# MLP of a decoder trunk on one core: two products accumulate on in the banks of two others, five sums per pair in place of seven, and the products with a weight piece's remainder come last

## The chip, the core and the metric

The kernel runs on 1 core of one Trainium2 chip. The metric is the device time of one execution in microseconds (us). Three timed runs of the kernel before gave 2285.32 to 2286.46 us, with a median of 2285.71 us. Lower is better.

## What is computed

The reference is a decoder trunk of two layers over 256 tokens of width 2048: attention with an MLP behind it, then a state-space mixer with another MLP behind it. The change lies in the MLP alone, which runs twice:

```python
D_MODEL, SEQ, D_FF = 2048, 256, 8192

def squared_relu_mlp(h, w_in, w_out):      # h: (256, 2048), after an RMS norm
    u = jax.nn.relu(h @ w_in)              # (256, 8192)
    return (u * u) @ w_out                 # (256, 2048), added to the residual stream
```

All tensors are float32. The kernel keeps the precision by splitting each operand in two: a rounded part and the remainder, `(ah, al)` of the activations and `(wh, wl)` of the weights. A product of two operands is then three matmuls, `ah·wh + al·wh + ah·wl`, into one float32 accumulator.

## The kernel before, in words

**Weight pieces.** Weights come from HBM in pieces of 128x1024 float32 (512 KB: two blocks of 128 rows by 512 columns). The SP queue loads each into a raw buffer (`wraw`, six of them; `wrx`, four more in the MLP). ScalarE (ACT) rounds the piece into `wh` (L102), VectorE (DVE) subtracts to get the remainder `wl` (L103), and TensorE (PE) takes both. There are four `wh` and four `wl` buffers. `Flow.next` (L124) hands one piece to PE and converts up to three pieces ahead, so each piece goes DMA, ACT, DVE, PE. The PE program stands in the order of the code. The order on ACT and DVE is made by a scheduler when the program is built.

**The first matmul of the MLP.** The hidden layer is made in 16 column blocks of 512, taken two at a time: a pair `p` holds the blocks `2p` and `2p+1`. Pair 0 is computed straightforwardly (tokens of kind "c"). Pairs 1 to 7 use a 2x2 scheme of the Strassen kind: the tokens are cut into two halves of 128, the 2048 inputs into two halves of 1024, the pair into its two blocks, and seven products of half size stand for eight. They are called M1, N7, N5, N6, N4, M2, N3. Each takes four pieces (d = 0 to 3, tokens of kind "s") and accumulates over them in a PSUM bank of its own, six from the four banks of the pool `acc` in turn and N7 from the pool `sm`. In the profile a bank of such a product is called `st`. The activations that they multiply (sums and differences of the input's quarters) are made once per layer by `combinations`; the weights that they multiply are made from the loaded quarters by `seven`: DVE adds (L183) and, for two of them, adding DMAs of the GpSimd queue (L199).

**The sums behind the products.** When a product's fourth piece is done, `after` (L627) queues what can be made: ACT copies M1 out of its bank (L630); after N5 and N6, DVE makes w = N6 − m1, c = N5 + w, w = N7 + w and e = N7 + c (L636 to L639); after N4 it makes w − N4, after M2 it adds M2 to m1, after N3 it adds N3 to c. These are seven DVE sums per pair (L620 and L621 are the helpers that the profile names). e, w − N4, m1 + M2 and c + N3 are the four quarters of the pair's hidden values. Each goes through a Relu on ACT (L624), a square (L566), and a transposition on PE, whose result is split into `k` tiles (L299 on ACT, L300 on DVE) for the second matmul.

**The second matmul.** Tokens of kind "o" multiply the hidden values of an earlier pair with four pieces of the output weights, both token halves at once, into two banks of the pool `yp`; DVE then adds the result to the residual (L436). `merged` (L1415) mixes the "s" tokens of a pair with the "o" tokens of the pairs before it into one order, by a rough model of time, and `plan` (L1460) strings the pairs together. Neither is touched by the change.

**The products of one piece.** `products` (L609) issues the matmuls of one piece: six for an "s" token, twelve for a "c" or "o" token. Its order is, for each of the two row blocks and each accumulator: ah·wh (L616), ah·wl (L617), al·wh (L618). Outside these tokens, `block` (L328) does the same work in another order: all products with `wh` of the piece (L339, L340), then those with `wl` (L343).

Of the kernel before, what the change touches and what calls it, by code (L numbers as in the profile page):

```python
# [23 lines left out]
AF = mybir.ActivationFunctionType  # L24
# [5 lines left out]
S = 256  # L30
# [184 lines left out]
class Trunk:  # L215
# [343 lines left out]
    def mlp_body(self, mp, layer, gain):  # L559
        nc = self.nc  # L560
        xa, rs = self.xT, self.rs
        us = {}

        def hidden(r, pp, j, t):

            nc.scalar.activation(r, r, AF.Square)  # L566
            if (pp, j) not in us:
                us[pp, j] = (self.ktile(self.k4), self.ktile(self.k4))
            h, lo = us[pp, j]
            if by_words(pp, j, t):  # L570
                r = self.words(r, 3, mp)
            return lambda wide: self.transposes(r, h, lo, t, wide)

        def relu(src, t):
            r = self.scratch()
            nc.scalar.activation(r, src, AF.Relu, scale=rs[t])
            return r

        def lhs_x(kt, t):
            return [v[:, kt % 8] for v in xa[kt // 8, t]]  # L580

        def lhs_u(pp):
            return self.from_tiles([us[pp, 0], us[pp, 1]])

        S, steps = self.combinations(mp, xa)
        S["M1"], S["N4"], S["M2"] = xa[0, 0], xa[1, 1], xa[1, 0]
        out, bank, v, count = {}, {}, {}, {}
        due = []
        at = [0.0, 0.0]

        def when(us, fn):
            due.append((at[0] + us, fn))

        def move(us):
            at[0] += us
            for e in [e for e in due if e[0] <= at[0]]:
                due.remove(e)
                e[1]()

        def turn(r, p, j, t, us):  # L600

            fn = hidden(r, p, j, t)
            at[1] = max(at[0] + us + (COPY if by_words(p, j, t) else 0), at[1] + TR_GAP)
            due.append((at[1], lambda: fn(False)))

        def pair_of_banks(pool):
            return [pool.tile([P, 512], F32, tag=pool.name, name=self.name(pool.name)) for _ in range(2)]

        def products(accs, key, lhs, kt, first, last):  # L609
            u, (h, lo) = self.flow.next(key)  # L610
            for q in range(2):
                k = 2 * kt + q
                wh, wl = h[:, q * 512:(q + 1) * 512], lo[:, q * 512:(q + 1) * 512]
                for t, b in enumerate(accs):
                    ah, al = lhs(k, t)
                    nc.tensor.matmul(b, ah, wh, start=first and q == 0, stop=False)  # L616
                    nc.tensor.matmul(b, ah, wl, start=False, stop=False)  # L617
                    nc.tensor.matmul(b, al, wh, start=False, stop=last and q == 1)  # L618

        sub = lambda o, a, b: nc.vector.tensor_tensor(o, a, b, ALU.subtract)  # L620
        plus = lambda o, a, b: nc.vector.tensor_tensor(o, a, b, ALU.add)  # L621

        def relu_in_place(r, t):
            nc.scalar.activation(r, r, AF.Relu, scale=rs[t])  # L624
            return r

        def after(name, p):  # L627
            if name == "M1":
                v["m1"] = self.scratch()
                nc.scalar.activation(v["m1"], bank["M1"], AF.Copy)  # L630
            elif name in ("N5", "N6"):
                v[name] = p
                if v.get("N5") != p or v.get("N6") != p:
                    return
                w, c, e = (self.scratch() for _ in range(3))
                sub(w, bank["N6"], v["m1"])  # L636
                plus(c, bank["N5"], w)
                plus(w, bank["N7"], w)
                plus(e, bank["N7"], c)  # L639
                v["w"], v["c"] = w, c  # L640
                turn(relu_in_place(e, 1), p, 1, 1, TR[0])
            elif name == "N4":
                sub(v["w"], bank["N4"], v["w"])
                turn(relu_in_place(v["w"], 1), p, 0, 1, TR[1])
            elif name == "M2":
                plus(v["m1"], bank["M2"], v["m1"])
                turn(relu_in_place(v["m1"], 0), p, 0, 0, TR[2])
            elif name == "N3":
                plus(v["c"], bank["N3"], v["c"])
                turn(relu_in_place(v["c"], 0), p, 1, 0, TR[3])  # L650

        tokens = plan()
        inside = False
        when(5, steps[0])
        when(10, steps[1])
        for tok in tokens:
            key = (tok[0], layer) + tok[1:]
            if tok[0] == "s":
                _, p, name, d = tok
                if not inside:  # L660
                    inside = True
                    self.flow.ahead = (6, 3)
                if count.setdefault(name, 0) % 4 == 0:
                    pool = self.sm if name == "N7" else self.acc
                    bank[name] = pool.tile([P, 512], F32, tag=pool.name, name=self.name("st"))
                count[name] += 1
                products([bank[name]], key, lambda k, t: [x[:, k] for x in S[name]], d,
                         count[name] % 4 == 1, count[name] % 4 == 0)
                if count[name] % 4 == 0:
                    after(name, p)  # L670
                move(1.36)
            elif tok[0] == "c":
                _, p, j, o = tok
                if o == 0:
                    out["c"] = pair_of_banks(self.yp if j else self.acc)
                products(out["c"], key, lhs_x, o, o == 0, o == 7)
                if o == 7:
                    for t in range(2):
                        turn(relu(out["c"][t], t), p, j, t, TR[4])
                    if j:  # L680
                        when(3, steps[2])
                if o % 2:
                    self.tick()
                move(2.72)
            else:
                _, p, nb, o = tok
                if o == 0:
                    out[nb] = pair_of_banks(self.yp)
                products(out[nb], key, lhs_u(p), o, o == 0, o == 3)
                if o == 3:  # L690
                    self.add_residual(nb, out.pop(nb))
                move(2.72)
        move(1e9)
        assert not self.queue
        if gain is not None:
            self.boundary_begin(gain)
        for nb in range(4):
            keys = [("mo", layer, 7, nb, q) for q in range(2)]
            if gain is None and nb == 3:
                self.last_block(keys, lhs_u(7))  # L700
                break
            accs = self.block(keys, lhs_u(7))
            if gain is not None:
                self.finalize(nb, accs)
            else:
                for t in range(2):
                    self.result(t, nb, slice(0, 512), accs[t])
        if gain is not None:
            self.boundary_end()
# [694 lines left out]
TR = (10, 8, 7, 7, 5)  # L1404
# [4 lines left out]
def by_words(p, j, t):  # L1409

    return 0 < p < 7
# [48 lines left out]
def plan():  # L1460

    out = [("c", 0, 0, o) for o in range(8)]
    for p in range(1, 8):
        first = [(("o", p - 2, 3), 4)] if p > 1 else [(("c", 0, 1), 8)]
        out += merged(p, first + [(("o", p - 1, nb), 4) for nb in range(4 if p == 7 else 3)])
    return out
# [139 lines left out]
```

## Time and profile before

| what | value |
|---|---|
| timed runs, median (lowest to highest) | 2285.71 us (2285.32 to 2286.46) |
| span of the profiled execution, first to last instruction | 2284.5 us |
| PE busy | 2278.1 us, 10929 matmuls |
| DVE busy | 1915.9 us |
| ACT busy | 1390.1 us |
| granted TensorE clock | 1.000 |
| HBM read | 529.65 MB |

For the profiled execution the profile gives no other time of its own than this span; the median of the timed runs is 1.2 us above it, which is what lies before the first and behind the last instruction together with the spread of the runs (1.1 us).

How to read it: PE rows are matmuls, PEld rows are the loads of their stationary operand, which overlap the matmul before. Matmuls are pipelined, so a matmul's own duration (about 0.39 us) is longer than the distance from one start to the next (about 0.23 us), and the busy time of PE does not tell by itself whether it runs at its best. The idle time before an instruction is listed with what ended it.

### The profile page before, as it was taken

The page shows a single profiled execution, that of the slowest core. Times are in us where ns is not written, and L with a number is a line of the kernel's source. Part 1 is how long each engine was busy: PE and PEld are TensorE (multiplying, and loading weights), DVE is VectorE, ACT ScalarE, POOL GpSimd, SP SyncE. Part 2 cuts the span into 40 slices and gives each one's busy share as a digit, 9 for nine tenths or more (in the row PEclk, how much of TensorE's full clock was granted, in tenths as well). Part 3 has the DMA queues.
Part 4 walks back from the last instruction along what each step waited for, and adds up shares of the span by engine and source line. Part 5 has one row for each costly group of instructions (what it writes and reads, how often), then busy time and mean ns, then how long its engine had stood idle before and what let it go on. Part 6 is the DMA issues. An engine that isn't in the chain of part 4 may idle for free.

```text
span 2284.5 us, 30768 instructions
## 1 busy us (share of the span) xinstructions
PE 2278.1 (100%) x10929; PEld 1889.6 (83%) x10929; DVE 1915.9 (84%) x2318; ACT 1390.1 (61%) x1947; POOL 275.5 (12%) x315
## 2 busy tenths in 40 slices
PE   9999999999999999999999999999999999999999
PEld 7898888888888888888888888888888888888887
DVE  7786698999898897687899688676989889989985
ACT  7775576566666666564666555545666666666663
POOL 1440000000000000100133213121000000000000
PEclk9999999999999999999999999999999999999999
DMA  8545678888888878667888787767688888888874
GB/s 315 173 153 159 211 230 267 259 255 270 264 255 259 267 232 271 227 208 241 277 280 278 245 275 264 229 222 229 204 265 248 259 270 253 260 275 247 267 232 160
DMA packets 167706, 557.16 MB, mean 244 GB/s; under 512 B 19040, under 2 KB 28192, under 8 KB 166528
## 3 DMA queue, kind: packets, MB, share of 16 engines
q1 hardware_dynamic: 151264, 502.44, 66.2%
q0 software_dynamic: 13888, 48.49, 10.0%
q10 hardware_dynamic: 2400, 4.27, 0.5%
q8 instruction: 86, 1.41, 0.3%
q14 instruction: 68, 0.56, 0.1%
HBM read 529.65 MB, written 6.41 MB: 235 GB/s over the span
## 4 chain that ended last, share of the span: by engine, by line
PE 96%; DVE 1%; DMA 1%; ACT 1%; issue 1%; POOL 0%; SPq 0%; ACTq 0%; DVEq 0%
PE acc L339 13%; PE acc L340 13%; PE acc L343 13%; PE yp L618 9%; PE yp L617 9%; PE yp L616 9%; PE st L617 7%; PE st L618 7%; PE st L616 7%; DMA wraw<-mi 1%; PE sm L324 1%; DVE wl L103 1%; PE y L1309 1%; PE sm L322 1%; PE acc L616 1%; PE acc L618 1%
## 5 line engine op out<-in xcount | busy, mean ns | idle before, releaser
L102 ACT ACTIVATE wh<-wraw 128x1024 fp32r<-128x1024 f32 (+1 forms) x818 | 856.2, 1053 | 570.4 <-PE acc L340 268.9
L103 DVE TENSOR_TENSOR wl<-wraw,wh 128x1024 fp32r<-128x1024 f32 (+1 forms) x818 | 985.5, 1221 | 240.6 <-ACT wh L102 216.6
L616 PE MATMUL yp<-wh,k 128*128 128x512 f32 x896 | 349.2, 390 | 0.0
L618 PE MATMUL yp<-wh,k 128*128 128x512 f32 x896 | 348.8, 389 | 0.0
L617 PE MATMUL yp<-wl,k 128*128 128x512 f32 x896 | 348.6, 389 | 0.0
L339 PE MATMUL acc<-wh,xt 128*128 128x512 f32 x704 | 279.7, 397 | 0.4 <-ACT wh L102 0.4
L340 PE MATMUL acc<-wh,xt 128*128 128x512 f32 x704 | 274.9, 390 | 0.1
L102 ACT ACTIVATE wh<-wrx 128x1024 fp32r<-128x1024 f32 x168 | 177.8, 1058 | 153.4 <-PE yp L618 101.7
L103 DVE TENSOR_TENSOR wl<-wrx,wh 128x1024 fp32r<-128x1024 f32 x168 | 204.3, 1221 | 36.6 <-ACT wh L102 35.6
L618 PEld LDWEIGHTS yp<-wh,k 128*128 128x128 f32 x896 | 168.2, 188 | 35.1
L617 PEld LDWEIGHTS yp<-wl,k 128*128 128x128 f32 x896 | 168.2, 188 | 34.9
L616 PEld LDWEIGHTS yp<-wh,k 128*128 128x128 f32 x896 | 168.2, 188 | 34.8
L339 PE MATMUL acc<-wh,k 128*128 128x512 f32 x496 | 196.5, 396 | 0.0
L340 PE MATMUL acc<-wh,k 128*128 128x512 f32 x496 | 193.3, 390 | 0.0
L343 PE MATMUL acc<-wl,xt 128*128 128x512 f32 x704 | 188.3, 389 | 0.0
L616 PE MATMUL st<-wh,xt 128*128 128x512 f32 x448 | 177.7, 397 | 0.0
L618 PE MATMUL st<-wh,xt 128*128 128x512 f32 x448 | 174.9, 390 | 0.0
L617 PE MATMUL st<-wl,xt 128*128 128x512 f32 x448 | 174.7, 390 | 0.0
L339 PEld LDWEIGHTS acc<-wh,xt 128*128 128x128 f32 x704 | 132.7, 188 | 29.4 <-ACT wh L102 1.6
L340 PEld LDWEIGHTS acc<-wh,xt 128*128 128x128 f32 x704 | 132.5, 188 | 28.5 <-issue 1.2
L343 PEld LDWEIGHTS acc<-wl,xt 128*128 128x128 f32 x704 | 132.1, 188 | 27.7
L199 POOL DMA_DIRECT2D wrx<-mi x56 | 49.2, 878 | 720.6 <-DVE wl L103 524.5
(318 smaller groups left out, 3527.0 us busy)
## 6 DMA issues: line engine op xcount, KB each, us to landing
wraw<-mi SPq DMA_DIRECT2D x256, 512.0 KB, 5.5
wraw<-mo SPq DMA_DIRECT2D x256, 512.0 KB, 5.6
wraw<-si SPq DMA_DIRECT2D x160, 512.0 KB, 5.2
wraw<-so SPq DMA_DIRECT2D x64, 512.0 KB, 5.2
wrx<-mi SPq DMA_DIRECT2D x56, 512.0 KB, 5.4
wrx<-mi POOLq DMA_DIRECT2D x56, 512.0 KB, 7.8
wraw<-wo SPq DMA_DIRECT2D x32, 512.0 KB, 4.0
taps<-xD SPq DMA_DIRECT2D x16, 768.0 KB, 8.4
```

The lines of the kernel that those rows point to most:

```text
L102: self.last = nc.scalar.activation(h[:, v], raw[:, v], AF.Copy)
L103: self.last_lo = nc.vector.tensor_tensor(lo[:, v], raw[:, v], h[:, v].bitcast(F32), ALU.subtract)
L199: nc.gpsimd.dma_start(st["b11"].tile, quarter(d, 1, 0), accum_op=ALU.add)
L322: self.nc.tensor.transpose(b.bitcast(F32R)[:, v], words[:, v], self.ident_r)
L324: self.nc.tensor.transpose(b[:, v], src[:, v], self.ident)
L339: nc.tensor.matmul(accs[t][:, :n], ah, wh[:, q, :], start=first and kt + q == 0, stop=False)
L340: nc.tensor.matmul(accs[t][:, :n], al, wh[:, q, :], start=False, stop=False)
L343: nc.tensor.matmul(accs[t][:, :n], lhs(kt + q, t)[0], wl[:, q, :], start=False, stop=en and q == nk - 1)
L616: nc.tensor.matmul(b, ah, wh, start=first and q == 0, stop=False)
L617: nc.tensor.matmul(b, ah, wl, start=False, stop=False)
L618: nc.tensor.matmul(b, al, wh, start=False, stop=last and q == 1)
L1309: nc.tensor.matmul(y[t][c, o], part(t)[:, c], xg[g][t][:, o], start=True, stop=True)
```

## The change

The diff has two parts.

```diff
         def products(accs, key, lhs, kt, first, last, more=False):
             u, (h, lo) = self.flow.next(key)
+            half = lambda w, q: w[:, q * 512:(q + 1) * 512]
             for q in range(2):
-                k = 2 * kt + q
-                wh, wl = h[:, q * 512:(q + 1) * 512], lo[:, q * 512:(q + 1) * 512]
                 for t, b in enumerate(accs):
-                    ah, al = lhs(k, t)
-                    nc.tensor.matmul(b, ah, wh, start=first and q == 0, stop=False)
-                    nc.tensor.matmul(b, ah, wl, start=False, stop=False)
-                    nc.tensor.matmul(b, al, wh, start=False, stop=last and q == 1)
+                    ah, al = lhs(2 * kt + q, t)
+                    nc.tensor.matmul(b, ah, half(h, q), start=first and q == 0, stop=False, skip_group_check=more)
+                    nc.tensor.matmul(b, al, half(h, q), start=False, stop=False, skip_group_check=more)
+            for q in range(2):
+                for t, b in enumerate(accs):
+                    nc.tensor.matmul(b, lhs(2 * kt + q, t)[0], half(lo, q), start=False, stop=last and q == 1,
+                                     skip_group_check=more)
...
-                w, c, e = (self.scratch() for _ in range(3))
+                w, g, e = (self.scratch() for _ in range(3))
                 sub(w, bank["N6"], v["m1"])
-                plus(c, bank["N5"], w)
-                plus(w, bank["N7"], w)
-                plus(e, bank["N7"], c)
-                v["w"], v["c"] = w, c
+                plus(g, bank["N7"], w)
+                plus(e, bank["N5"], g)
+                v["w"], v["g"] = w, g
                 turn(relu_in_place(e, 1), p, 1, 1, TR[0])
             elif name == "N4":
-                sub(v["w"], bank["N4"], v["w"])
-                turn(relu_in_place(v["w"], 1), p, 0, 1, TR[1])
+                sub(v["g"], bank["N4"], v["g"])
+                turn(relu_in_place(v["g"], 1), p, 0, 1, TR[1])
             elif name == "M2":
-                plus(v["m1"], bank["M2"], v["m1"])
-                turn(relu_in_place(v["m1"], 0), p, 0, 0, TR[2])
+                nc.scalar.activation(v["m1"], bank["M1"], AF.Relu, scale=rs[0])
+                turn(v["m1"], p, 0, 0, TR[2])
             elif name == "N3":
-                plus(v["c"], bank["N3"], v["c"])
-                turn(relu_in_place(v["c"], 0), p, 1, 0, TR[3])
+                plus(v["w"], bank["N5"], v["w"])
+                turn(relu_in_place(v["w"], 0), p, 1, 0, TR[3])
...
-                if count.setdefault(name, 0) % 4 == 0:
+                onto = {"M2": "M1", "N3": "N5"}.get(name, name)
+                if count.setdefault(name, 0) % 4 == 0 and onto == name:
...
-                products([bank[name]], key, lambda k, t: [x[:, k] for x in S[name]], d,
-                         count[name] % 4 == 1, count[name] % 4 == 0)
+                products([bank[onto]], key, lambda k, t: [x[:, k] for x in S[name]], d,
+                         count[name] % 4 == 1 and onto == name, count[name] % 4 == 0, onto != name)
```

First, `products` issues all products with `wh` of a piece and then those with `wl`, as `block` does. Second, M2 accumulates on in the bank of M1, and N3 in that of N5: M1's bank is read by the copy in the middle and by a Relu of ACT at the end, so that M1 + M2 needs no DVE sum; N5's bank is read by e = N5 + g in the middle and by w + (N5 + N3) at the end, so that c is not made. Five sums are left, and a pair takes four `acc` banks in place of six. `skip_group_check` adds no instruction.

On PE the order within a piece changes. This is the first N6 piece of the fourth pair in the first layer (`st` is N6's bank, `sN` the activations' two parts, `wh` and `wl` the piece), before:

```order
L616 MATMUL st_5600<-wh_5551,sN_428_3186 128x512
L617 MATMUL st_5600<-wl_5552,sN_428_3186 128x512
L618 MATMUL st_5600<-wh_5551,sN_429_3187 128x512
L616 MATMUL st_5600<-wh_5551,sN_428_3186 128x512
L617 MATMUL st_5600<-wl_5552,sN_428_3186 128x512
L618 MATMUL st_5600<-wh_5551,sN_429_3187 128x512
```

and with the change:

```order
L615 MATMUL st_5588<-wh_5539,sN_428_3186 128x512
L616 MATMUL st_5588<-wh_5539,sN_429_3187 128x512
L615 MATMUL st_5588<-wh_5539,sN_428_3186 128x512
L616 MATMUL st_5588<-wh_5539,sN_429_3187 128x512
L619 MATMUL st_5588<-wl_5540,sN_428_3186 128x512 x2
```

The piece's remainder was read by the second matmul and is now first read by the fifth. In a piece of the "o" kind, with twelve matmuls, it was the second and is now the ninth.

On DVE the sums behind N5 and N6 of the third pair in the first layer (`s` is a scratch tile, `st` a bank: N6, N5, N7, N7 in turn) stood so before, between pieces' remainders:

```order
L620 TENSOR_TENSOR s_519_5266<-st_4893,s_518_5194 128x512
L103 TENSOR_TENSOR wl_5281<-wraw_5222,wh_5280 128x1024
L621 TENSOR_TENSOR s_520_5267<-st_4880,s_519_5266 128x512
L103 TENSOR_TENSOR wl_5295<-wraw_5234,wh_5294 128x1024
L621 TENSOR_TENSOR s_519_5266<-st_4838,s_519_5266 128x512
L621 TENSOR_TENSOR s_521_5268<-st_4838,s_520_5267 128x512
```

and stand so now (N6, N7, N5):

```order
L622 TENSOR_TENSOR s_515_5258<-st_4885,s_514_5186 128x512
L103 TENSOR_TENSOR wl_5271<-wraw_5214,wh_5270 128x1024
L623 TENSOR_TENSOR s_516_5259<-st_4830,s_515_5258 128x512
L103 TENSOR_TENSOR wl_5285<-wraw_5226,wh_5284 128x1024
L623 TENSOR_TENSOR s_517_5260<-st_4872,s_516_5259 128x512
```

One sum of the four is gone; the second one that goes, behind M2, stood further on.

Where the fourth pair begins, DVE adds weight quarters (L183) and makes the first remainders of N5 (`wl` out of the `wraw` of the row with `wrx,wraw` at its left) and of N6 (`wl` out of `wrx`). Before, the rows from N5's add to N6's remainder were:

```order
L183 TENSOR_TENSOR wraw_5446<-wrx_5434,wraw_5446 128x1024
L183 TENSOR_TENSOR wraw_5548<-wraw_5546,wraw_5548 128x1024
L300 TENSOR_TENSOR k_529_5386<-sm_5524,k_528_5385 128x4x128
L103 TENSOR_TENSOR wl_5536<-wraw_5446,wh_5535 128x1024
L183 TENSOR_TENSOR wrx_5434<-wrx_5434,wraw_5448 128x1024
L183 TENSOR_TENSOR wraw_5546<-wrx_5532,wraw_5546 128x1024
L103 TENSOR_TENSOR wl_5552<-wrx_5434,wh_5551 128x1024
```

and with the change:

```order
L183 TENSOR_TENSOR wraw_5434<-wrx_5422,wraw_5434 128x1024
L183 TENSOR_TENSOR wraw_5536<-wraw_5534,wraw_5536 128x1024
L183 TENSOR_TENSOR wrx_5422<-wrx_5422,wraw_5436 128x1024
L300 TENSOR_TENSOR k_524_5376<-sm_5512,k_523_5375 128x4x128
L103 TENSOR_TENSOR wl_5524<-wraw_5434,wh_5523 128x1024
L103 TENSOR_TENSOR wl_5540<-wrx_5422,wh_5539 128x1024
```

N6's add has moved ahead of a transposition's remainder and of N5's remainder, and the add for the next N5 piece, which stood ahead of N6's remainder, has moved behind it. Outside the two MLPs the order on every engine is as before.

More of the change, by code (lines that the diff above doesn't have):

```diff
@@ L607, in pair_of_banks, with products @@
             return [pool.tile([P, 512], F32, tag=pool.name, name=self.name(pool.name)) for _ in range(2)]
-        def products(accs, key, lhs, kt, first, last):
+        def products(accs, key, lhs, kt, first, last, more=False):
             u, (h, lo) = self.flow.next(key)
+            half = lambda w, q: w[:, q * 512:(q + 1) * 512]
             for q in range(2):
-                k = 2 * kt + q
-                wh, wl = h[:, q * 512:(q + 1) * 512], lo[:, q * 512:(q + 1) * 512]
                 for t, b in enumerate(accs):
-                    ah, al = lhs(k, t)
-                    nc.tensor.matmul(b, ah, wh, start=first and q == 0, stop=False)
-                    nc.tensor.matmul(b, ah, wl, start=False, stop=False)
-                    nc.tensor.matmul(b, al, wh, start=False, stop=last and q == 1)
+                    ah, al = lhs(2 * kt + q, t)
[5 more added lines that the diff above has]
+                                     skip_group_check=more)
         sub = lambda o, a, b: nc.vector.tensor_tensor(o, a, b, ALU.subtract)
```

## The prediction

> **What bounds the kernel now.** The page comes first: the busy times, the clock, and the chain of work that ended last.
>
> ```profile
> PE 2278.1 (100%) x10929; PEld 1889.6 (83%) x10929; DVE 1915.9 (84%) x2318; ACT 1390.1 (61%) x1947; POOL 275.5 (12%) x315
> PEclk9999999999999999999999999999999999999999
> PE 96%; DVE 1%; DMA 1%; ACT 1%; issue 1%; POOL 0%; SPq 0%; ACTq 0%; DVEq 0%
> ```
>
> TensorE is occupied throughout at its full granted clock, and 96% of the chain is its own work. Then the windows of the two MLPs' tokens, the only places that the change touches (columns: us, then busy us and count of PE, PEld, DVE, ACT, POOL, then clock):
>
> ```profile
> 283.00:914.00 631.00, 630.83 (x2850) 520.45 (x2849) 569.64 (x557) 401.84 (x433) 38.19 (x53) 1.00 0.84 257
> 1617.00:2249.00 632.00, 631.90 (x2853) 520.90 (x2852) 570.04 (x558) 401.97 (x433) 37.59 (x52) 1.00 0.83 255
> ```
>
> PE has no idle time here, but its rows can hide waiting, since a matmul's row grows when its operand is late. So the waits of the weight load (us in total, times, longest) are the view that says what the change can win:
>
> ```profile
> PEld st L617 <- DVE wl L103: 3.2, 8, 0.5
> PEld yp L617 <- DVE wl L103: 0.5, 2, 0.3
> ```
>
> L617 is the first product with the remainder. In both MLPs together, PE waits for DVE ten times, 3.7 us of 2284.5, and for nothing else of note. DVE is 90% busy in these windows (570 of 631), so it is the second limit, but one with 61 us to spare in each.
>
> **The change part by part.** *The products.* Their number stays. Whether the new order costs PE anything by itself is shown by `block`, which has it already (L339, L340, L343 against L616 to L618):
>
> ```profile
> L339 PE MATMUL acc<-wh,k 128*128 128x512 f32 x496 | 196.5, 396 | 0.0
> L340 PE MATMUL acc<-wh,k 128*128 128x512 f32 x496 | 193.3, 390 | 0.0
> L343 PE MATMUL acc<-wl,k 128*128 128x512 f32 x496 | 132.7, 389 | 0.0
> L616 PE MATMUL st<-wh,xt 128*128 128x512 f32 x448 | 177.7, 397 | 0.0
> L617 PE MATMUL st<-wl,xt 128*128 128x512 f32 x448 | 174.7, 390 | 0.0
> L618 PE MATMUL st<-wh,xt 128*128 128x512 f32 x448 | 174.9, 390 | 0.0
> L616 PE MATMUL st<-wh,sN 128*128 128x512 f32 x336 | 133.0, 396 | 0.0
> ```
>
> 396, 390, 389 ns stand against 397, 390, 390: no difference in either direction. I take 0.
>
> *The remainder last.* The worst of the ten waits, at the first N6 piece of the fourth pair, in the timeline of PE, of its loads, of DVE and of ACT:
>
> ```profile
> 569.32 0.39 PE L618 MATMUL st<-wh,sN 128*128 128x512 f32 x1
> 569.55 0.40 PE L616 MATMUL st<-wh,sN 128*128 128x512 f32 x1
> 570.01 0.50 PE L617 MATMUL st<-wl,sN 128*128 128x512 f32 x1
> 570.35 0.40 PE L618 MATMUL st<-wh,sN 128*128 128x512 f32 x1
> ```
> ```profile
> 570.01 0.19 PEld L617 LDWEIGHTS st<-wl,sN 128*128 128x128 f32 x1 [0.50 <-DVE wl L103]
> ```
> ```profile
> 564.59 0.68 DVE L300 TENSOR_TENSOR k<-sm,k 128x512 fp32r<-128x512 f32 x1
> 566.33 1.22 DVE L183 TENSOR_TENSOR wrx<-wrx,wraw 128x1024 f32<-128x1024 f32 x1
> 568.73 1.23 DVE L103 TENSOR_TENSOR wl<-wrx,wh 128x1024 fp32r<-128x1024 f32 x1
> ```
> ```profile
> 567.64 1.06 ACT L102 ACTIVATE wh<-wrx 128x1024 fp32r<-128x1024 f32 x1 [3.58 <-DVE wrx L183]
> ```
>
> Starts are 0.23 us apart (569.32 to 569.55). Here the next two distances are 0.46 and 0.34, so PE lost 0.23 + 0.11 = 0.34 us of the 0.50 that its load stood idle; 0.16 of each idle belongs to the normal rhythm. Over all ten: 3.7 − 10 x 0.16 = 2.1 us lost. The new order reads the remainder three products later in an "s" piece (0.69 us) and seven later in an "o" piece (1.6 us). The worst loss is 0.34 us, so all ten go: −2.1 us. What is late next at this place is `wh`: it was done at 568.70, 0.85 us ahead of its matmul, and nothing makes it later, since DVE's add before it has moved ahead of two steps (an L300 of 0.68 and an L103 of 1.22 us). For that N5's remainder moves back by one add (1.22 us). The timeline of PE around N5's first product, with the transposes before it:
>
> ```profile
> 568.02 0.30 PE L324 MATMUL sm<-ident,s 128*128 128x128 f32 x1
> 568.08 0.48 PE L616 MATMUL st<-wh,sN 128*128 128x512 f32 x1
> 568.39 0.40 PE L617 MATMUL st<-wl,sN 128*128 128x512 f32 x1
> ```
>
> N5's remainder was started at 565.19 and ended at 566.41:
>
> ```profile
> 565.19 1.22 DVE L103 TENSOR_TENSOR wl<-wraw,wh 128x1024 fp32r<-128x1024 f32 x1
> ```
>
> It would now end at about 567.6 and be needed about 0.7 us after 568.39, at 569.1: 1.5 us are left, cost 0.
>
> *Buffers.* In a piece, `wh` is read last two or four products earlier, `wl` one product later (0.23 us). DVE's remainders wait for ACT, not for a free `wl`, so the later release costs 0; the earlier one helps ACT, which is not late:
>
> ```profile
> DVE wl L103 <- ACT wh L102: 252.2, 247, 3.7
> ```
>
> *Sums and Relus.*
>
> ```profile
> L621 DVE TENSOR_TENSOR s<-st,s 128x512 f32<-128x512 f32 x70 | 46.7, 684 | 0.1
> L624 ACT ACTIVATE s<-s,rs 128x512 f32<-128x512 f32 x56 | 40.2, 718 | 17.8 <-DVE s L621 11.4 <-DVE s L620 6.4
> L630 ACT ACTIVATE s<-st 128x512 f32<-128x512 f32 x14 | 8.4, 598 | 3.7 <-PE st L618 3.7
> ```
>
> Two of five L621 per pair go, 28 in all: 28 x 0.684 = 19.2 us of DVE's 1140 in these windows. ACT's Relu behind M2 reads a bank as L630 does: 14 x (718 − 598) = 1.7 us off ACT. Both lie beside PE's work, which fills the windows: 0 on the path, apart from the waits already counted.
>
> *The held banks.* M1's bank is now free only after the Relu behind M2, N5's only after the sum behind N3, and the next pair takes them up. Last product of N3 (PE), its sum (DVE) and the Relu behind M2 (ACT) at the end of the third pair, then M1's first product of the fourth:
>
> ```profile
> 556.31 0.39 PE L618 MATMUL st<-wh,xt 128*128 128x512 f32 x1
> ```
> ```profile
> 558.80 0.68 DVE L621 TENSOR_TENSOR s<-st,s 128x512 f32<-128x512 f32 x1
> ```
> ```profile
> 553.60 0.71 ACT L624 ACTIVATE s<-s,rs 128x512 f32<-128x512 f32 x1
> ```
> ```profile
> 562.24 0.48 PE L616 MATMUL st<-wh,xt 128*128 128x512 f32 x1
> ```
>
> The fourth pair's M1 begins at 562.24, 7.9 us after that Relu's end; its N5 begins at 568.08, 8.6 us after that sum's end. Within a pair M2 now waits for the copy of M1 and N3 for e. N3 follows e most closely in the seventh pair: the last sums there and N3's first product.
>
> ```profile
> 878.66 1.28 DVE L621 TENSOR_TENSOR s<-st,s 128x512 f32<-128x512 f32 x2
> ```
> ```profile
> 882.99 0.39 PE L616 MATMUL st<-wh,xt 128*128 128x512 f32 x1
> ```
>
> 3.05 us, and e now comes one sum earlier. None of the four waits has a price while these margins hold: 0. [...]
>
> *The sum.* 0 − 2.1 + 0 + 0 = −2.1 us against the profiled span of 2284.5, so a span of 2282.4. The median of the timed runs stands 1.2 us above the span, hence 2283.6 us. Ends: at best the whole 3.7 us of idle load go, and what PE's rows lie above 389 ns at L617 and L618 (about 1 us): −4.8, or 2280.9. At worst nothing goes and the run lies at the top of the spread shown, 2286.4.
>
> **The rivals.** *The wait moves, nothing is won (2285.7).* At N6 the chain behind the remainder runs through DVE's add of the next N7 piece, which waits for its DMA (0.54 us idle):
>
> ```profile
> 563.45 1.23 DVE L183 TENSOR_TENSOR wraw<-wraw,wraw 128x1024 f32<-128x1024 f32 x1 [0.54 <-DMA wraw<-mi]
> ```
>
> If DVE, relieved, only stands longer before this row, everything behind it comes at the old time. Against it: even at the old time the remainder is needed 0.69 us later. It wins only if N6's `wh` also comes 0.85 us later. Chance 0.12.
>
> *The held banks bite: slower.* If a sum behind N3 sits in DVE's queue until the next pair's N5 wants its bank, PE stands, and with it everything behind on its in-order queue. It decides from 8.6 us of lateness, seven steps of 1.22 us. One step too many costs 1.2 us at each of the 12 places where a pair follows a pair: +14.6, less 2.1, or 2298.2. For it: the scheduler has moved this sum behind one more remainder. Against it: it ends 3.2 us after N3's last product starts, about a quarter of the 11.8 us until the next N5. Chance 0.05.
>
> *DVE is the true limit: faster.* At 90% in both windows DVE might pace PE through many small delays that no wait shows; then the 19.2 us of sums come off the time: 2266.5. Against it stand PE's loads, whose ten short waits are all that they show, and ACT, which itself waits for PE to free `wh` buffers, so that the conversions run ahead of PE and not behind it:
>
> ```profile
> ACT wh L102 <- PE yp L618: 260.3, 172, 1.7
> ```
>
>  Chance 0.06, with the upper reach of my own sum.
>
> **How the numbers follow.** My forecast has 0.77; the three rivals 0.12, 0.05 and 0.06. About 0.2%, 4.6 us, is what a measurement of this kernel can tell from no change. Forecast and first rival both lie within it: same 0.89, slower 0.05, faster 0.06. The range takes the ends of the sum, 2280.9 to 2286.4, which hold the forecast and the first rival; it leaves out the two outer ones, 0.11.
>
> **What would show it right or wrong.** Right: the weight load's waits for DVE at the first product with `wl` (now L619) are gone or under 1 us in total; L623 counts 42 and DVE's busy time falls by some 19 us without the span following; ACT's new Relu at L647 takes about 0.6 us; the M1 and N5 products that begin a pair show no wait for ACT or DVE. Wrong: waits of PE for `wh` at N6 pieces (first rival); waits at the first M1, N5, M2 or N3 product, or PE busy below the window's length (second); a span that falls by far more than the listed waits (third).

## The result, and the profile after

The change made the kernel slower: 2303.41 us as the median of five runs (2299.1 to 2305.4), against 2285.71 before; ratio 1.0075, 95% interval 1.0062 to 1.0087. The forecast was 2283.6. The page of the profiled execution, whose own time is 2303.41 us and its span 2301.6 us:

```profile
PE 2281.3 (99%) x10929; PEld 1889.6 (82%) x10929; DVE 1897.7 (82%) x2290; ACT 1391.8 (60%) x1947; POOL 276.4 (12%) x315
PE 96%; DMA 2%; DVE 1%; issue 1%; ACT 0%; POOL 0%; DVEq 0%; SPq 0%; ACTq 0%
```

DVE lost 18 us of work, as it should, and the span grew by 17. The windows of the two MLPs (same stretches as before):

```profile
283.00:914.00 631.00, 622.91 (x2808) 512.18 (x2808) 555.02 (x538) 398.65 (x430) 38.19 (x53) 1.00 0.83 254
1617.00:2249.00 632.00, 625.94 (x2819) 514.88 (x2818) 558.43 (x543) 400.49 (x434) 39.44 (x55) 1.00 0.83 252
```

PE is no longer busy throughout, and it gets through fewer matmuls in the same stretch (2808 for 2850, 2819 for 2853). What it waits for, first PE's own rows, then its loads':

```profile
PE yp L615 <- DVE x L436: 12.6, 8, 2.2
PE yp L619 <- DVE wl L103: 1.1, 1, 1.1
```
```profile
PEld yp L615 <- issue: 11.0, 7, 2.6
PEld yp L615 <- ACT wh L102: 5.1, 3, 1.8
PEld yp L619 <- DVE wl L103: 1.5, 1, 1.5
PEld st L619 <- DVE wl L103: 0.2, 1, 0.2
```

Most of the waits that the prediction counted on have gone: the loads' 3.7 us for the remainder, at ten places, are 1.7 at two. In their place stands one that was not there: the first product of an "o" group waits for L436, the residual sums that read the two `yp` banks of the group before it. (The loads' rows for L615 are in the main the same gaps seen once more, since each of these loads starts 0.03 us ahead of its matmul.) And DVE itself waits longer than before for a load from HBM, first before, then after:

```profile
DVE wraw L183 <- DMA wraw<-mi: 18.1, 27, 2.0
```
```profile
DVE wraw L183 <- DMA wraw<-mi: 50.9, 29, 3.7
```

The add of a coming N7 piece (L183) waits for its quarter from HBM. One such place shows how the two belong together. It is the third pair of the first layer, on DVE, before the change:

```profile
509.83 1.23 DVE L103 TENSOR_TENSOR wl<-wraw,wh 128x1024 fp32r<-128x1024 f32 x1
510.98 1.28 DVE L436 TENSOR_TENSOR x<-yp,x 128x512 f32<-128x512 f32 x2
514.25 1.23 DVE L183 TENSOR_TENSOR wraw<-wraw,wraw 128x1024 f32<-128x1024 f32 x1 [2.00 <-DMA wraw<-mi]
```

and after it, then PE at the same time:

```profile
509.49 1.22 DVE L103 TENSOR_TENSOR wl<-wraw,wh 128x1024 fp32r<-128x1024 f32 x1
514.21 1.22 DVE L183 TENSOR_TENSOR wraw<-wraw,wraw 128x1024 f32<-128x1024 f32 x1 [3.50 <-DMA wraw<-mi]
515.35 1.28 DVE L436 TENSOR_TENSOR x<-yp,x 128x512 f32<-128x512 f32 x2
```
```profile
513.39 0.61 PE L619 MATMUL st<-wl,sN 128*128 128x512 f32 x2
516.18 0.47 PE L615 MATMUL yp<-wh,k 128*128 128x512 f32 x1 [2.17 <-DVE x L436]
```

The quarter lands at the same moment, 514.2, in both kernels. Before, DVE had its residual sums behind it by then and waited 2.0 us for nothing that PE needed. Now the add stands ahead of the sums in DVE's queue; DVE stands 3.5 us, the sums come 4.4 us later, and PE stands 2.17 us for its banks. The load itself began only at 507.33; in the chain of the change it stands directly behind a remainder of DVE, the step that reads a raw buffer last. That it waited for the buffer is read from the chain, no run tests it alone.

```profile
506.08 1.23 DVE wl L103
507.33 6.75 DMA wraw<-mi
```

DVE keeps the order of its queue at this place: it stands idle from 510.71 to 514.21 and begins the sums only after the add, although the products that they read ended at 511.29 (the last L619 into `yp`).

Counted over the queue's order, the N7 add stands directly ahead of residual sums at 10 places of the change (the same pattern of rows), and at none before, where it stood directly behind them at 10. Seven of PE's eight waits for residual sums, 1.2 to 2.2 us each, are at these places; the eighth, 0.3 us, is elsewhere. At the other three places, where the add waits 1.3 to 1.6 us, PE does not wait.

These waits make up most of the 17.1 us. The parts, as an estimate: 12.6 us idle; some 0.3 us more at each of the eight, since at the place shown the distance from the second L619's start, about 513.6 (513.39 + 0.61 − 0.39), to 516.18 is 2.6 us in place of 0.23 and the next starts are a little late as well, 2.5 in all; 1.1 us at one remainder; and 1.6 us of a lower clock (below). Less the 2.1 us that should have been won by the prediction's working, that is 15.7; the remaining 1.4 are not assigned.

### The profile page after: what moved, and what is told of

It is laid out like the page before. It is cut to its first block, busy times and chain, and to the rows that moved or that the text cites. A ratio compares the mean times of both kernels' runs of the same rounds, so it can differ in the third digit from the quotient of the medians.

```text
span 2301.6 us, 30974 instructions
## 1 busy us (share of the span) xinstructions
PE 2281.3 (99%) x10929; PEld 1889.6 (82%) x10929; DVE 1897.7 (82%) x2290; ACT 1391.8 (60%) x1947; POOL 276.4 (12%) x315
## 4 chain that ended last, share of the span: by engine, by line
PE 96%; DMA 2%; DVE 1%; issue 1%; ACT 0%; POOL 0%; DVEq 0%; SPq 0%; ACTq 0%
PE acc L339 13%; PE acc L340 13%; PE acc L343 13%; PE yp L615 9%; PE yp L619 9%; PE yp L616 9%; PE st L615 7%; PE st L616 7%; PE st L619 7%; DMA wraw<-mi 1%; PE sm L324 1%; PE sm L322 1%; PE y L1311 1%; PE acc L615 1%; PE acc L616 1%; PE acc L619 1%
## 5 line engine op out<-in xcount | busy, mean ns | idle before, releaser
L615 PE MATMUL yp<-wh,k 128*128 128x512 f32 x896 | 351.7, 393 | 12.7 <-DVE x L436 12.6
L619 PE MATMUL yp<-wl,k 128*128 128x512 f32 x896 | 239.9, 389 | 1.1 <-DVE wl L103 1.1
L615 PEld LDWEIGHTS yp<-wh,k 128*128 128x128 f32 x896 | 168.6, 188 | 53.6 <-issue 11.0
L619 PEld LDWEIGHTS yp<-wl,k 128*128 128x128 f32 x896 | 168.3, 188 | 36.6 <-DVE wl L103 1.5
L615 PE MATMUL st<-wh,xt 128*128 128x512 f32 x448 | 177.7, 397 | 0.0
L619 PE MATMUL st<-wl,xt 128*128 128x512 f32 x448 | 138.0, 389 | 0.0
```

The costliest lines, as they stand in the source:

```text
L615: nc.tensor.matmul(b, ah, half(h, q), start=first and q == 0, stop=False, skip_group_check=more)
L619: nc.tensor.matmul(b, lhs(2 * kt + q, t)[0], half(lo, q), start=False, stop=last and q == 1, skip_group_check=more)
```

## The experiments

Theory A: the cost is the place of one instruction. An N7 add that waits for its DMA stands in DVE's queue ahead of something that PE needs next. Theory B, the prediction's second rival: the held banks of M1 and N5 cost. Where a ratio is given, it is to the kernel before, in runs on the same chip.

**The two halves apart.** e1 takes only the new `products`, e2 only the rest of the change:

```diff
 # e1: before, with
+            for q in range(2):
+                for t, b in enumerate(accs):
+                    nc.tensor.matmul(b, lhs(2 * kt + q, t)[0], half(lo, q), ...)
 # e2: the change, with the order of before
+                    nc.tensor.matmul(b, ah, wh, start=first and q == 0, stop=False, skip_group_check=more)
+                    nc.tensor.matmul(b, ah, wl, start=False, stop=False, skip_group_check=more)
+                    nc.tensor.matmul(b, al, wh, start=False, stop=last and q == 1, skip_group_check=more)
```

> The first half of the change alone: products with the remainder last, all seven sums and all banks as before. In the order of its DVE queue the add for a coming N7 piece stands directly ahead of the residual sums of an o group at 10 places, as with the whole change, where before it stood directly behind them. Theory A (the add waits for its DMA and holds up the residual sums behind it, which hold the yp banks): 2298 to 2306 us, waits of PE for the residual sums of 10 us or more. Theory B (the held banks of M1 and N5 are the cause): no held banks here, so 2283 to 2285 us, no such waits.

> The second half of the change alone: M2 and N3 continue in the banks of M1 and N5, five sums per pair, the products in the order of before. Its DVE queue has the residual sums ahead of the N7 add at all 10 places, as before. Theory A: 2284 to 2287 us, PE waits for the remainder at L617 of some 3 us as before, none for the residual sums. Theory B: 2300 us or more.

e1: 2301.99 us, ratio 1.0070 (1.0056 to 1.0084). e2: 2321.39 us, ratio 1.0139 (1.0124 to 1.0155). e1 came out as theory A has it: no bank is held, DVE has all its seven sums, and the same waits are there. The new order of the products is thus enough by itself to bring the add ahead of the sums.

```profile
PE yp L615 <- DVE x L436: 11.2, 9, 2.3
```

e2 was a miss for A as it was stated, since the residual sums were ahead of the add there, and by its number a point for B. Its waits, however, are not at a bank:

```profile
PE st L617 <- DVE wl L103: 27.8, 10, 3.5
```

PE waits for the remainder of the last N3 piece. On DVE, before N3 ends in the second pair, first of the kernel before, then of e2:

```profile
468.75 0.69 DVE L621 TENSOR_TENSOR s<-st,s 128x512 f32<-128x512 f32 x1
469.35 0.68 DVE L300 TENSOR_TENSOR k<-sm,k 128x512 fp32r<-128x512 f32 x1
469.94 2.35 DVE L103 TENSOR_TENSOR wl<-wraw,wh 128x1024 fp32r<-128x1024 f32 x2
```
```profile
469.41 0.69 DVE L300 TENSOR_TENSOR k<-sm,k 128x512 fp32r<-128x512 f32 x1
473.87 1.22 DVE L183 TENSOR_TENSOR wraw<-wraw,wraw 128x1024 f32<-128x1024 f32 x1 [3.77 <-DMA wraw<-mi]
475.02 3.49 DVE L103 TENSOR_TENSOR wl<-wraw,wh 128x1024 fp32r<-128x1024 f32 x3
```

The first row of before is M2's sum, which e2 lacks. The add has moved ahead of three remainders, stands 3.77 us for its DMA, and the remainder that PE reads at its next matmul lies behind it. That is the mechanism of A at another place. It widens A (ahead of whatever PE needs next) and had to be tested by itself, below. In the whole change the add stands ahead of these three remainders too, but at this one it waits 1.56 us in place of 3.77, the remainder is read by later products, and PE's list has no wait of this kind.

**The add behind the sums.** e3 is the whole change, with the add queued behind the last residual sum:

```diff
-                add("b22", "b12", "b22")
+                with flow.tc.issue_after(flow.last_add.ins) if flow.last_add else nullcontext():
+                    add("b22", "b12", "b22")
...
-            self.nc.vector.tensor_tensor(x, accs[t], x, ALU.add)
+            self.flow.last_add = self.nc.vector.tensor_tensor(x, accs[t], x, ALU.add)
```

> The whole change, with each N7 add tied behind the last residual sum that the program issued before it; nothing else is added. Theory A: the waits of PE for the residual sums go, 2282 to 2287 us, which is the 2283.6 of the prediction. Theory B: the banks are held as in the change, so it stays at 2300 to 2306 us.

2283.91 us, ratio 0.9985 (0.9976 to 0.9993). PE's waits for residual sums are gone; of those for a remainder one is left (lines lie one to three further on here: L104 is the remainder, L184 the add, L438 the residual sum, L622 the product with `wl`):

```profile
PE yp L622 <- DVE wl L104: 0.7, 1, 0.7
```

The held banks are the same as in the change, so B falls as the cause of the 17 us. On DVE, at the place shown above:

```profile
510.64 1.29 DVE L438 TENSOR_TENSOR x<-yp,x 128x512 f32<-128x512 f32 x2
511.85 2.35 DVE L104 TENSOR_TENSOR wl<-wraw,wh 128x1024 fp32r<-128x1024 f32 x2
514.23 1.23 DVE L104 TENSOR_TENSOR wl<-wrx,wh 128x1024 fp32r<-128x1024 f32 x1
515.37 1.22 DVE L184 TENSOR_TENSOR wraw<-wraw,wraw 128x1024 f32<-128x1024 f32 x1
```

The sums are back at 510.6, and the add, at 515.4, finds its quarter there.

**More loads in flight.** e4 is the whole change with two more `wrx` buffers, and the first of N7's two quarters goes there. It was to make the load land earlier and leave the order alone:

```diff
-            for name, n in (("rx", 4), ("ry", 1)):
+            for name, n in (("rx", 6), ("ry", 1)):
-B12 = "raw"
+B12 = "rx"
```

> The whole change, with the first of the two N7 quarters loaded into the wrx pool, which gets six buffers in place of four, so that more loads are in flight; the DVE queue still has the N7 add ahead of the residual sums at the 10 places. Theory A: it is the DMA's landing that costs, not the place in the queue; with the landing earlier DVE's idle time at the add falls from 3.5 us to under 1 us, and the time to 2282 to 2290 us. Rival C (the add's own 1.2 us ahead of the residual sums is the cost): stays at 2296 us or more. Theory B: stays at 2300 us or more.

2291.21 us, ratio 1.0021 (1.0012 to 1.0030): a little over A's range, well under that of C and B. But the order did not stay. With the quarter in `wrx`, the N7 add is the row `wraw<-wrx,wraw` and the N5 add is `wrx<-wrx,wrx`. Around the same place:

```profile
506.55 1.23 DVE L183 TENSOR_TENSOR wraw<-wrx,wraw 128x1024 f32<-128x1024 f32 x1 [1.29 <-DMA wraw<-mi]
514.51 1.22 DVE L183 TENSOR_TENSOR wrx<-wrx,wrx 128x1024 f32<-128x1024 f32 x1
515.64 1.28 DVE L436 TENSOR_TENSOR x<-yp,x 128x512 f32<-128x512 f32 x2
```

The add ahead of the sums is now N5's, which waits for no load; N7's has gone to 506.55, and over the run it still waits 23.4 us, up to 3.4 at once. Over the whole queue N7's add stands directly ahead of residual sums at 2 places in place of 10, and N5's at 12 in place of 2. So e4 changed the landing and the place together, does not separate them, and does not show that the landing alone is the cost. What it does show speaks against C: an add of 1.2 us that does not wait may stand ahead of the sums at little cost, since PE's waits for residual sums fall from 12.6 to 2.1 us. PE also waits 2.8 us for two remainders here, and the 4.8 us (0.21%) by which e4 still lies above the kernel before are not split further.

**A wider tie, a miss.** e5 to e8 tie the add behind the last residual sum and behind the last remainder that the program issued before it: e5 in the second half alone, e6 in the first half, e7 in the kernel before, e8 in the whole change.

```diff
+                with flow.tc.issue_after(flow.last_add.ins) if flow.last_add else nullcontext():
+                    with flow.tc.issue_after(flow.last_lo.ins):
+                        add("b22", "b12", "b22")
```

> The second half alone (held banks, five sums, products in the order of before), with each N7 add tied behind both the last residual sum and the last remainder that the program issued before it. Theory A, widened after the banks-only run (an N7 add that waits for its DMA in DVE's queue, ahead of whatever PE needs next): PE's wait for the remainder of the last N3 piece (27.8 us in all without the tie) goes, and the time comes to 2284 to 2289 us. Theory B (the held banks themselves cost): it stays at 2300 us or more.

> The first half alone (remainder last, seven sums, six banks), with the same tie. Theory A: the waits for the residual sums go and what the prediction counted for the remainder comes out: 2 to 4 us under the kernel before, 2282 to 2285 us. If the order of the products had a cost of its own on PE, it stays above the kernel before.

> The kernel before with the same tie and nothing else. Theory A: there the add stood behind the residual sums already, so the tie has little to mend: within 3 us of the kernel before. If the tie were worth something by itself, and not only against the displaced add, this falls by the same 3 us as the whole change with the add behind the residual sums did.

> The whole change with the tie to the last residual sum and the last remainder. Theory A: no wait of PE for a residual sum, 2281 to 2285 us, not slower than with the tie to the residual sum alone. If DVE now stands still elsewhere (its adds come later and the products made from them too), 2286 us or more.

2300.98 us (ratio 1.0067, 1.0054 to 1.0081), 2293.13 (1.0029, 1.0018 to 1.0041), 2298.04 (1.0052, 1.0040 to 1.0065) and 2292.93 (1.0030, 1.0018 to 1.0041). All four missed what A expected; e5 lies where B had it, and e8 where its second guess had it (the adds come later, and the products made from them too). The tie has a price of its own: the control, e7, is 11.6 us slower than the untied kernel. The adds are moved further back, and PE now waits at N5, N6 and N7 pieces, those whose weights are made by adds (PE in e7, where L620 and L621 are the first two products of a piece):

```profile
PE st L621 <- DVE wl L104: 4.6, 12, 0.8
PE st L620 <- ACT wh L103: 2.4, 2, 1.2
```

These waits are 7.0 of the 11.6 us; the rest is not split. So these four decide nothing between A and B by their distance to the kernel before. One part of A's expectation for e5 did come: the 27.8 us of waits for the last N3 piece's remainder are gone, and its list has the rows of e7 and 2.0 us of waits for residual sums besides. Among themselves, with e7 as the base, the new order of products (e6) is 4.9 us faster and the second half (e5) 2.9 us slower; on top of the new order (e8 against e6) the second half makes no difference, 0.2 us. The lesson is that the add must come neither too early nor too late.

**The sum put back, the sum alone taken out.** e9 is e2 with a DVE sum that nobody reads, at the place of M2's. e11 is the kernel before without M2's sum: the Relu reads M2's own bank, so M1 is left out of that quarter, and nothing else changes.

```diff
 # e9: the second half alone, with
+                plus(self.scratch(), bank["M1"], v["m1"])
                 nc.scalar.activation(v["m1"], bank["M1"], AF.Relu, scale=rs[0])
 # e11: before, with
-                plus(v["m1"], bank["M2"], v["m1"])
-                turn(relu_in_place(v["m1"], 0), p, 0, 0, TR[2])
+                nc.scalar.activation(v["m1"], bank["M2"], AF.Relu, scale=rs[0])
+                turn(v["m1"], p, 0, 0, TR[2])
```

> The second half alone (held banks, products in the order of before), and behind M2 one DVE sum whose result nobody reads, at the place and of the size of the sum that went. In the order of DVE's queue the N7 add is then back behind the three remainders that it had overtaken in the banks-only run. Theory A: 2285 to 2288 us, level with the kernel before, and PE's wait of 27.8 us for the last N3 piece's remainder gone, although DVE has 9.6 us more work than in the banks-only run. Theory B (the held banks cost): it stays above 2300 us.

> The kernel before with only the DVE sum behind M2 left out: the Relu reads M2's own bank, so M1 is not added (part of the computation is left out). No bank is held, the products are as before, and DVE has 9.6 us less to do. In its queue the N7 add has moved ahead of three remainders, as in the banks-only run. Theory A: as slow as the banks-only run, 2310 to 2325 us, with PE waiting some 28 us for the last N3 piece's remainder. Theory B: 2284 to 2287 us, since nothing of the held banks is there.

e9: 2285.95 us, ratio 0.9997 (0.9989 to 1.0006). e11: 2324.32 us, ratio 1.0165 (1.0152 to 1.0179). PE's waits for the remainder in e9, then in e11:

```profile
PE st L617 <- DVE wl L103: 1.5, 3, 0.8
```
```profile
PE st L617 <- DVE wl L103: 28.8, 10, 3.9
```

Both came out as A has it. With the dummy sum the add is back behind the three remainders, and the kernel is 35 us faster than e2 by the medians (of two chips); the same sum taken out of the kernel before made it 38 us slower, with all banks as before. That settles it: the held banks cost nothing that can be measured (e9), and what cost in e2 was the add that took the sum's place.

**The remainder last, by itself.** e10 is e1 with e3's tie.

> The first half alone (remainder last, seven sums, six banks), with each N7 add tied behind the last residual sum only. Its queue still has another N7 add ahead of residual sums at 8 other places. Theory A: the 11 us of waits for residual sums at the 10 places go, 2282 to 2288 us; as far as the 8 places wait for a DMA, nearer to the upper end. If the order of products costs PE something itself: 2295 us or more.

2284.13 us, ratio 0.9990 (0.9981 to 0.9999). No wait for a residual sum is left in its list, and the new order has no cost on PE that shows. (At the 8 other places that the expectation names, the row ahead of the sums is an N5 add, which waits for no load.)

**Both remedies.** e12 is e3 with the buffers of e4.

> The whole change with the N7 add tied behind the last residual sum, and the first N7 quarter in the wrx pool of six buffers. If DVE's remaining waits for the quarters' DMA (17.2 us in the run with the tie alone) still cost PE anything, it comes to 2281 to 2283.5 us; if PE has nothing left to win but its steps at semaphores, it stays within 1 us of the run with the tie alone (0.9985 of the kernel before).

2283.80 us, ratio 0.9990 (0.9982 to 0.9999), level with e3. DVE's waits for the quarters fall from 17.2 to 4.6 us, in e3 and e12,

```profile
DVE wraw L184 <- DMA wraw<-mi: 17.2, 17, 3.3
```
```profile
DVE wraw L184 <- DMA wraw<-mi: 4.6, 9, 0.8
```

and the time changes by nothing that the interval can tell: in these runs a wait of DVE cost only where PE needed what lay behind it. No run shows by themselves the steps of PE at semaphores that the expectation names. e3, e10 and e12 all lie 0.10% to 0.15% under the kernel before, with intervals that end just below 1.

## Why the prediction was wrong

The terms of its sum are borne out as far as the runs can tell, once the add is tied. The products' new order costs PE nothing that shows (e10 is under the kernel before). The ten waits for the remainder were worth 2.1 us by the working; e10 measures 0.10% or 2.3 us (0.2 to 4.3), e3 0.15% or 3.4 us (1.6 to 5.5). Both carry the tie, whose own effect no run gives, and the intervals are wide, so that 2.3 comes so near to 2.1 is partly luck. The held banks cost nothing that shows: e9, which has them, is at 0.9997 of the kernel before (0.9989 to 1.0006). The 19.2 us off DVE were worth 0 on the path: DVE's busy time fell by 18 and the span did not follow. The step from span to time, 1.2 us, was a little short: in the runs on record the time is about 1.8 us above the same run's span.

The step that failed is the one on the moved instructions, which went into the sum at nothing. The prediction read the new DVE order at one place, the start of a pair, found N6's add earlier there and wrote that "nothing makes it later"; it took the rest of the scheduler's order as harmless. Some forty rows ahead of that place, the N7 add had been moved ahead of the residual sums, and this was to be seen in the order before any run. What stands in its place is 12.6 us of PE idle behind that add, most of the 17.1. The first rival did name the row that waits for its DMA, but priced it wrongly: "everything behind it comes at the old time" holds for what stood behind it before, and not for the sums that now stood behind it for the first time. Part of the price was at hand too. Before, the add already stands 2.0 us for a load that lands at 514.2; sums moved from before it to behind it cannot come ahead of that landing, and the wait grows to 3.5 us because DVE no longer has the sums to do first.

Behind the narrow range stood the thought that less work on a busy engine costs nothing at worst. Two runs answer it. e1 takes no work off DVE, has the add ahead of the sums at the same number of places and is about as slow as the change, so the missing sums are not needed for the loss; and e11 shows that one sum less can be enough, where the order of DVE's queue is made anew: there the add stands 3.31 us for its DMA, at 472.58, ahead of three remainders, and PE waits 28.8 us in all for remainders.

Of the signs that the prediction gave, DVE's 18 us, the 42 rows of L623 and the missing waits at the M1 and N5 products came; the loads' waits for the remainder did not fall under 1 us but to 1.7. The rival "held banks bite" had the right sign, and one of its signs came as well, PE busy below the window's length; it was the wrong mechanism all the same, since no wait stands at a first M1, N5, M2 or N3 product and e3 is fast with the banks held. The third rival fell with its premise, since DVE's load fell by 18 us and the span grew by 17, with PE's waits at single rows of DVE (12.6 us behind the adds).

Why the scheduler placed the add so early is not shown by a run. e1 shows that the new order of the products decides it at the residual sums; e9 and e11 show that one sum of 0.68 us in the queue decides it at the last N3 remainder.

## What to carry to other kernels

When a change lets a scheduler order an engine's queue anew, compare the whole order for rows that wait for a DMA or another engine, and ask of each what is now behind it that was ahead of it before. Less work on an engine can make the kernel slower (e11, 38 us), because the row that fills the gap may be one that waits (3.31 us at the place named above); tie that one row behind what must not wait, and no further, since e7's wider tie cost 11.6 us. A test that puts the removed work back as a dummy tells a lost place in the queue from a true cost.

## What the runs showed of the hardware

PE's clock fell after one short wait and not after two others of about the same length. In the profiled run of the change, PE stood idle for 2.17 us up to 516.18, for 2.15 us up to 1859.90 and for 2.24 us up to 2032.01. The stretches around the first wait, then around the second (PE's busy time is the second number, the granted clock the third from the right):

```profile
511.78:515.19 3.41, 2.22 (x10) 1.50 (x8) 0.98 (x1) 2.12 (x2) 0.00 (x0) 1.00 0.93 262
515.19:518.61 3.42, 2.43 (x10) 1.91 (x11) 3.42 (x5) 0.25 (x1) 0.00 (x0) 1.00 0.80 218
```
```profile
1856.63:1860.05 3.42, 1.27 (x6) 0.76 (x6) 2.12 (x3) 1.46 (x2) 0.00 (x0) 1.00 0.99 271
1860.05:1863.46 3.41, 3.41 (x9) 2.62 (x10) 3.41 (x4) 0.00 (x0) 0.00 (x0) 0.50 0.70 185
1863.46:1866.87 3.41, 3.41 (x17) 2.80 (x16) 3.38 (x4) 1.60 (x2) 0.00 (x0) 1.00 0.86 265
```

Behind the second wait the granted clock is 0.50 for 3.41 us, and starts are 0.43 us apart in place of 0.23: 8 matmuls, 1.6 us. Around the third it stays at 1.00. The stretches are not chosen freely. In the traces of the change and of the kernel before, the clock changes only at whole multiples of 3.4133 us after its first rise to full: in the change that rise is at 6.61 us, and the changes at 1860.05, 1863.46 and, behind the last matmul, 2300.36 lie 543, 544 and 672 steps later; in the kernel before the rise is at 7.46 and the one change, behind the last matmul, at 2284.15, 667 steps later. The first wait lies across such an edge, 1.19 us on one side and 0.98 on the other, and so does the third, 0.95 and 1.29; the second lies in one step, 2.15 us of it. Between the rise and the last matmul of the change this is the only step that is followed by one at half the clock; the next in idle time, 1.45 us from 682.45, is followed by one at 1.00. (Idle is counted by PE's rows, whose ends are modelled.) So in this run waits of about 2.2 us had two prices, by where they fell. That is one fall of the clock; no run tests what brings it about.

In e2 the wait of 3.42 us up to 476.29 is followed by a granted clock of 0.55 from 476.80 to 480.60, and starts there are again 0.43 us apart (477.42 to 477.85). Its profiled run has a mean granted clock of 0.996 over a span of 2321.9 us; the missing part, 0.0035 to 0.0045 before rounding, is 8 to 10 us of that span, as an estimate, beside its 27.8 us of waits.
